# Feed-forward nets in three passes of 256 columns, and x-side tiles at another start address

## The chip, the cores and the metric

The kernel runs on one core of one Trainium2 chip. The metric is the device time of one execution in microseconds (us); 1 us is 1000 ns. The core has a matmul engine (TensorE, PE in the profile; its weight loads stand under PEld), VectorE (DVE), ScalarE (ACT), GpSimd (POOL) and SyncE (SP, which here issues the transfers of the weights). Matmul operands are read from the on-chip memory SBUF, which has 128 partitions, and sums are gathered in PSUM banks of 512 float32 columns.

## The reference

A sequence of 256 positions of width 1024 runs through two blocks of two layers each. In the first block a layer is a mixer (pooling with attention, then a gated recurrence) and a feed-forward net; in the second block it is three attentions with gates, a feed-forward net and a gated side input. Everything is float32. The two nets, cut to what matters:

```
def conv_ffn(h, w_in, conv_w, conv_b, w_out):            # first block, 2 layers
    z = causal_dwconv(h @ w_in, conv_w, conv_b)          # h: 256 x 1024, w_in: 1024 x 5632
    u, g = jnp.split(z, 2, axis=-1)
    return (jax.nn.gelu(g) * u) @ w_out                  # w_out: 2816 x 1024

# second block, 2 layers
h = rms_norm_2(x, g_ffn)
a = depthwise_conv(h @ w_ffn_gate, conv_w, conv_b)       # 1024 x 2816
x = x + (jax.nn.gelu(a) * (h @ w_ffn_up)) @ w_ffn_down
```

## The kernel before

Every float32 product is made of three passes with operands in a rounded format (float32r): each operand is split into a high and a low part, and the sum is high*high + high*low + low*high. `mm3` (L277 to L281) issues the three, one line each: L279, L280, L281. One matmul has a stationary operand of 128x128, which a weight load brings into the array ahead of it, and a moving operand of up to 512 columns that streams past it.

The weights come as one stream of chunks of up to 128x2048, in the order of use. `_push` (L245 to L267) takes one chunk: SP issues the transfer into a tile `st`, ACT rounds it to `hi` (L262), DVE writes the rest to `lo` (L263), each in two halves. There are three buffers of each kind, and up to three chunks are prepared ahead of use (`AHEAD`).

On the other side of a product stands a tile with the normed activations. Before the change it is called `xx`: for each of 8 groups of 128 channels it holds 256 columns of high parts and, right behind them, 256 columns of low parts. `norm` and `first_norm` fill it and return its two halves `xh` and `xl`. The gated attention output (`o`, later again `xx`) and the hidden values of the nets (`hg`) are split in the same way. The text calls all of these the x-side tiles.

Two kinds of product occur. In a feature-major one (`fm_pair`, `fm_first`, `gate`, `branch`) the weights are stationary and the x-side tile moves, 256 columns a pass. In a token-major one (`tm_wide`, `tm_block`) the x-side tile is stationary and the weights move, mostly 512 columns a pass.

A net (`ffn`) has 22 blocks of 128 u and 128 g columns. A block is one chunk, 2 x 8 products of 128x128 by 256 columns, so 48 matmuls of 256 columns into one bank, T and S in turn. Then follow the norm's factor (`times_r`, DVE), the convolution, the gelu, the product with u and a split into `hg`. After every second block a token-major run `tm_wide` of 24 matmuls of 512 columns adds two blocks' share of the output to four banks A, A, A, O. The first two blocks of a net come together in `fm_first`, before the norm's factor is known.

In the two nets of the second block (`ffn_b`) blocks 3 to 17 take another form, `fm_wide` (L602 to L612): the high part of a weight moves past once with 512 columns, xh and xl together (L610), and the low part with the 256 columns of xh (L611). The 32 matmuls of such a block go into two banks, one of T and one of S, and `join` (L614 to L622) adds the two halves of each bank: two copies by ACT (L619), two adds by DVE (L620) and one multiply by DVE (L621).

Each tile tag has a fixed place in SBUF, given in the order in which tags are first used. `start` uses all large tags once, in a written order, so that order sets their addresses. Modulo 512 bytes per partition `st`, `hi` and `lo` start at 448. Behind them the small tags `ssx`, `ess` and `trcos` push the next ones on: `xx`, `w4`, `o`, `hg`, `w6`, `s`, `pT`, `qk`, `w2` and `bias` start at 128. A weight slice of 128 columns is 512 bytes and 256 columns are 1024, so slices of most chunks and all slices of x-side tiles keep these remainders. The exception is the chunk of 416 columns in `mla_prep`, whose rows are 1664 bytes, that is 3 x 512 + 128: its four groups of channels start at 448, 64, 192 and 320.

The order of the work on an engine is set by a scheduler from the program's order and its dependencies; in the attention part PE keeps the written order.

Of the kernel before, what the change touches and what calls it, by code (L numbers as in the profile page):

```python
# [12 lines left out]
F32R = mybir.dt.float32r  # L13
I32 = mybir.dt.int32
AF = mybir.ActivationFunctionType
ALU = mybir.AluOpType
# [3 lines left out]
P = 128  # L20
S = 256
D = 1024
KD = D // P
DFF = 2816
NF = DFF // P
# [4 lines left out]
CHUNK = 2048  # L30
# [179 lines left out]
class Net:  # L210
# [127 lines left out]
    def update(self, t, n, banks):  # L338
        xs = self.x[:, t, n * 512:n * 512 + 512]
        if banks is not None:  # L340
            self.nc.vector.tensor_tensor(out=xs, in0=banks[t][n][:, :], in1=xs, op=ALU.add)

    def first_norm(self):

        nc = self.nc
        self.xx = self.t([P, KD, 2 * S], "xx", F32R)
        xh, xl = self.xx[:, :, :S], self.xx[:, :, S:]
        ss = self.t([P, 2, 2], "ssx")
        copies = []
        for n in range(2):  # L350
            for t in range(2):
                pt = self.bank("ST"[t])
                for e in range(4):
                    k = 4 * n + e
                    self.pe.transpose(pt[:, e * P:e * P + P], self.x[:, t, k * P:k * P + P], self.ident)
                for e in range(4):
                    k = 4 * n + e
                    g = self.vec("gain0", k)
                    z, c = pt[:, e * P:e * P + P], slice(t * P, t * P + P)
                    copies.append(nc.scalar.activation(xh[:, k, c], z, AF.Copy, scale=g))  # L360
                    nc.vector.scalar_tensor_tensor(xl[:, k, c], z, g, xh[:, k, c].bitcast(F32), op0=ALU.mult, op1=ALU.subtract)
        for n in range(2):
            for t in range(2):
                sq = self.t([P, 512], "w2")
                self.after(nc.scalar.activation(sq, self.x[:, t, n * 512:n * 512 + 512], AF.Square, scale=1.0 / 32,
                                                accum_out=ss[:, n, t:t + 1]), copies)
        self.norm_r(ss)
        return xh, xl

    def norm(self, gi, banks=None, update=None):  # L370


        nc = self.nc
        update = update or self.update
        self.xx = self.t([P, KD, 2 * S], "xx", F32R)
        xh, xl = self.xx[:, :, :S], self.xx[:, :, S:]
        ss = self.t([P, 2, 2], "ssx")
        for n in range(2):
            for t in range(2):
                update(t, n, banks)  # L380
            for kp in range(2):
                pt = self.bank("ST"[kp])
                for e in range(2):
                    k = 4 * n + 2 * kp + e
                    for t in range(2):
                        self.pe.transpose(pt[:, e * S + t * P:e * S + t * P + P], self.x[:, t, k * P:k * P + P], self.ident)
                for e in range(2):
                    k = 4 * n + 2 * kp + e
                    g = self.vec(f"gain{gi}", k)
                    z = pt[:, e * S:e * S + S]  # L390
                    nc.scalar.activation(xh[:, k, :], z, AF.Copy, scale=g)  # L391
                    nc.vector.scalar_tensor_tensor(xl[:, k, :], z, g, xh[:, k, :].bitcast(F32), op0=ALU.mult, op1=ALU.subtract)
        for n in range(2):
            for t in range(2):
                sq = self.t([P, 512], "w2")
                nc.scalar.activation(sq, self.x[:, t, n * 512:n * 512 + 512], AF.Square, scale=1.0 / 32, accum_out=ss[:, n, t:t + 1])
        self.norm_r(ss)
        return xh, xl
# [48 lines left out]
    def start(self):  # L447
        nc, ap = self.nc, self.ap
        self.vecs = self.t(list(ap["vec"].shape), "vec")
        self.ident = self.t([P, P], "ident")  # L450
        g0 = self.vat["gain0"]
        self.act_o.dma_start(self.ident, ap["ident"])
        self.act_o.dma_start(self.vecs[:, g0:g0 + KD], ap["vec"][:, g0:g0 + KD])
        self.x = self.t([P, 2, D], "x")
        for tag, n in (("st", CHUNK), ("hi", CHUNK), ("lo", CHUNK), ("ssx", 4), ("ess", 4), ("trcos", 32)) + (("xx", 4 * D), ("w4", D), ("o", D), ("hg", 512), ("w6", 1536), ("s", 512), ("pT", 512), ("qk", 512), ("w2", 512), ("bias", 512)):
            self.t([P, n], tag)
        self.sync_o.dma_start(self.x[:, 0, :], ap["x"][:P, :])
        for _ in range(3):
            self._push()
        self.rows = self.t(list(ap["row"].shape), "row")  # L460
        self.ones = self.t([P, P], "ones")
        self.sync_o.dma_start(self.vecs[:, g0 + KD:], ap["vec"][:, g0 + KD:])
        self.sync_o.dma_start(self.ones, ap["ones"])
        self.sync_o.dma_start(self.rows, ap["row"])
        self.acc = None
# [133 lines left out]
        self.fm_pair(b, xh, xl, wh, wl, KD)  # L599
        return b  # L600

    def fm_wide(self):  # L602

        banks = [self.bank(tag) for tag in "TS"]
        wh, wl = self.chunk(KD, 256)
        mm = self.pe.matmul
        for e in range(2):
            for k in range(KD):
                c = slice(e * P, e * P + P)
                mm(banks[e], wh[:, k, c], self.xx[:, k, :], start=k == 0, stop=False)  # L610
                mm(banks[e][:, :S], wl[:, k, c], self.xx[:, k, :S], start=False, stop=k == KD - 1)  # L611
        return banks  # L612

    def join(self, z, banks):  # L614

        nc = self.nc
        y = self.t([P, 2, S], "w2")
        for e, b in enumerate(banks):
            nc.scalar.activation(y[:, e, :], b[:, S:], AF.Copy)  # L619
            nc.vector.tensor_tensor(out=z[:, e, :], in0=b[:, :S], in1=y[:, e, :], op=ALU.add)  # L620
        nc.vector.tensor_tensor(out=z, in0=z, in1=self.rb[:, None, :].to_broadcast([P, 2, S]), op=ALU.mult)  # L621
        return z  # L622

    def times_r(self, z, src):

        nc = self.nc
# [5 lines left out]
                                    in1=self.rb[:, None, :].to_broadcast([P, 2, S]), op=ALU.mult)  # L632
        return z

    def ffn(self, gi, body, aside=None, wide=False):
        xh, xl = self.norm(gi, self.acc)
        first = self.fm_first(xh, xl)
        self.norm_rows()
        acc = None
        done = []  # L640
        for j in range(NF):
            if aside is not None and 2 <= j < NF - 2:
                next(aside, None)
            if j % 2 == 0:
                hh, hl = self.t([P, 2, S], "hg", F32R), self.t([P, 2, S], "hg", F32R)
                done.append((hh, hl))
            z = self.t([P, 2, S], "s")
            if wide and 3 <= j < NF - 4:
                self.join(z, self.fm_wide())
            else:  # L650
                self.times_r(z, first[j] if j < 2 else self.fm(xh, xl, "TS"[j % 2]))
            m = body(j, z[:, 0, :], z[:, 1, :])
            self.split(hh[:, j % 2, :], hl[:, j % 2, :], m)
            if j % 2 and j > 2 * LAG:
                if acc is None:
                    acc = self.wide_banks()
                kk = j - 1 - 2 * LAG
                self.tm_wide(acc, *done[kk // 2], kk, False)
        for kk in range(NF - 2 * LAG, NF, 2):
            self.tm_wide(acc, *done[kk // 2], kk, kk == NF - 2)  # L660
        self.acc = acc
# [13 lines left out]
    def ffn_b(self, i, gi, aside):  # L675
        nc = self.nc

        def body(j, u, g):
            g = self.conv(g, f"cw{i}", f"cb{i}", j, 3, (1, 0, -1))
            nc.scalar.activation(g, g, AF.Gelu_apprx_tanh)  # L680
            nc.vector.tensor_tensor(out=g, in0=g, in1=u, op=ALU.mult)
            return g

        self.ffn(gi, body, aside, True)


    def softplus(self):
# [559 lines left out]
    def hybrid(self, i, g0):  # L1247
        nc = self.nc
        xh, xl = self.norm(g0, self.acc, self.pending)
        c, kr, skr = self.mla_prep(i, xh, xl)  # L1250
# [40 lines left out]

        def branch(b):
            if b == 2:
                mm = self.t([P, KD, 2 * S], "xx", F32R)
                mh, ml = self.halves = mm[:, :, :S], mm[:, :, S:]
            for jp in range(4):
                if jp % 2 == 0:
                    wh, wl = self.chunk(4, 512)
# [31 lines left out]
        for _ in branch(2):  # L1330
            pass
        mh, ml = self.halves
# [22 lines left out]
        xh, xl = self.norm(g0 + 2, self.acc)  # L1355
# [4 lines left out]
        e = [self.t([P, D], "w4") for _ in range(2)]  # L1360
# [10 lines left out]
        for t in range(2):  # L1371
            for n in range(2):
                c = slice(n * 512, n * 512 + 512)
# [49 lines left out]
```

## Time and profile before

| what | value |
|---|---|
| device time, median of 3 runs | 1484.84 us (1483.95 to 1485.08) |
| the profiled execution's own time | 1484.23 us |
| its span, first to last instruction | 1482.3 us |
| PE, PEld, DVE, ACT, POOL busy | 99%, 89%, 78%, 63%, 7% |
| matmuls | 9540 |
| mean DMA rate | 174 GB/s |
| granted TensorE clock | full (2.4 GHz) in every slice |

A matmul's duration in the profile includes a fixed latency; matmuls overlap. What a matmul costs the engine is the distance from its start to the next one's start, here called its pitch. A view of one matmul per row gives it, as the distance of two rows divided by the matmuls between them. The chain of waits is the list of steps, each released by the one before, that ends with the last instruction.

### The profile page before, as it was taken

What the parts mean: (1) busy time and instruction counts of PE and PEld (TensorE: products, weight loads), DVE (VectorE), ACT (ScalarE), POOL (GpSimd) and SP (SyncE); (2) the same over time, 40 slices, a digit from 0 to 9 for tenths busy, and PEclk for the clock granted to TensorE, in tenths of its full rate; (3) what the DMA queues carried; (4) which work ended last, traced back from release to release, by engine and by line L of the source; (5) the groups of instructions that cost most, each with busy time, mean ns of one, the idle gap of its engine ahead of it and who ended that gap; (6) DMA issues with size and microseconds to landing.
All of it is one profiled execution on the core that took longest, in us unless ns stands there. A gap on an engine that the chain in (4) does not pass through costs nothing.

```text
span 1482.3 us, 24541 instructions
## 1 busy us (share of the span) xinstructions
PE 1469.4 (99%) x9540; PEld 1312.3 (89%) x9540; DVE 1160.1 (78%) x2257; ACT 934.1 (63%) x1684; POOL 106.9 (7%) x101
## 2 busy tenths in 40 slices
PE   8999999999999999999999999999999999999998
PEld 6689999999999998899998988888899998988896
DVE  6669777789897877886877877778886877877766
ACT  7757555586666556765765755656766664765554
POOL 0200000000000000012530000000003250000000
PEclk9999999999999999999999999999999999999999
DMA  8455455444455554543335555544443435555551
GB/s 296 159 187 200 174 197 198 166 149 171 161 209 174 196 182 157 199 170 116 142 116 192 180 206 183 199 171 171 168 179 133 136 121 172 192 197 178 191 199 57
DMA packets 37877, 257.29 MB, mean 174 GB/s; under 512 B 4385, under 2 KB 4769, under 8 KB 8321
## 3 DMA queue, kind: packets, MB, share of 16 engines
q1 hardware_dynamic: 36576, 252.38, 47.9%
q0 software_dynamic: 896, 3.28, 0.6%
q8 instruction: 75, 1.23, 0.3%
q14 instruction: 42, 0.34, 0.1%
q10 hardware_dynamic: 288, 0.07, 0.0%
HBM read 254.66 MB, written 1.05 MB: 173 GB/s over the span
## 4 chain that ended last, share of the span: by engine, by line
PE 87%; DVE 8%; ACT 3%; issue 2%; DMA 0%; ACTq 0%
PE A L207 11%; PE A L280 9%; PE A L279 9%; PE A L281 9%; PE S L279 4%; PE S L281 4%; PE S L280 4%; PE T L279 4%; PE T L281 4%; PE T L280 4%; PE S L610 4%; PE T L610 4%; DVE lo L263 3%; PE T L611 2%; PE S L611 2%
## 5 line engine op out<-in xcount | busy, mean ns | idle before, releaser
L263 DVE TENSOR_TENSOR lo<-st,hi 128x1024 fp32r<-128x1024 f32 (+3 forms) x480 | 574.7, 1211 | 136.4 <-ACT hi L262 135.6
L262 ACT ACTIVATE hi<-st 128x1024 fp32r<-128x1024 f32 (+3 forms) x480 | 489.8, 1042 | 228.2 <-PE A L207 60.3
L281 PE MATMUL S<-xx,lo 128*128 128x256 f32 x496 | 139.4, 281 | 0.0
L279 PE MATMUL S<-xx,hi 128*128 128x256 f32 x496 | 139.2, 281 | 0.0
L280 PE MATMUL S<-xx,hi 128*128 128x256 f32 x496 | 139.1, 281 | 0.0
L207 PE MATMUL A<-xx,hi 128*128 128x256 f32 x768 | 138.8, 284 | 0.0
L279 PE MATMUL T<-xx,hi 128*128 128x256 f32 x480 | 135.6, 283 | 0.0
L280 PE MATMUL T<-xx,hi 128*128 128x256 f32 x480 | 135.0, 281 | 0.0
L281 PE MATMUL T<-xx,lo 128*128 128x256 f32 x480 | 134.8, 281 | 0.0
L207 PEld LDWEIGHTS A<-xx,hi 128*128 128x128 f32 x768 | 117.0, 188 | 8.2 <-issue 7.9
L281 PE MATMUL A<-hi,hg 128*128 128x512 f32 x294 | 115.6, 393 | 0.6 <-DVE hg L314 0.6
L279 PE MATMUL A<-hi,xx 128*128 128x512 f32 (+2 forms) x304 | 115.8, 383 | 0.2 <-ACT xx L391 0.2
L280 PE MATMUL A<-lo,hg 128*128 128x512 f32 x294 | 115.6, 393 | 0.0
L280 PE MATMUL A<-lo,xx 128*128 128x512 f32 (+2 forms) x304 | 115.3, 379 | 0.1
L279 PE MATMUL A<-hi,hg 128*128 128x512 f32 x294 | 115.1, 391 | 0.0
L281 PE MATMUL A<-hi,xx 128*128 128x512 f32 (+2 forms) x304 | 114.5, 379 | 0.0
L207 PE MATMUL A<-xx,lo 128*128 128x256 f32 x384 | 107.1, 279 | 0.0
L1115 POOL TENSOR_SCALAR s<-s,at 128x256 f32<-128x256 f32 x56 | 55.2, 1003 | 571.4 <-DVE at L960 570.8
L281 PEld LDWEIGHTS S<-xx,lo 128*128 128x128 f32 x496 | 94.6, 191 | 0.1
L279 PEld LDWEIGHTS S<-xx,hi 128*128 128x128 f32 x496 | 93.2, 188 | 0.1
L280 PEld LDWEIGHTS S<-xx,hi 128*128 128x128 f32 x496 | 93.2, 188 | 0.1
L281 PEld LDWEIGHTS T<-xx,lo 128*128 128x128 f32 x480 | 91.8, 191 | 0.0
(377 smaller groups left out, 3458.0 us busy)
## 6 DMA issues: line engine op xcount, KB each, us to landing
st<-in_w_dram SPq DMA_DIRECT2D x230, 1024.0 KB, 4.8
st<-in_w_dram SPq DMA_DIRECT2D x4, 832.0 KB, 4.9
st<-in_w_dram SPq DMA_DIRECT2D x2, 768.0 KB, 4.2
x<-in_x_dram SPq DMA_DIRECT2D x2, 512.0 KB, 5.1
st<-in_w_dram SPq DMA_DIRECT2D x4, 256.0 KB, 6.7
st<-in_w_dram SPq DMA_DIRECT2D x2, 512.0 KB, 3.5
w<-in_gain_dram POOLq DMA_DIRECT2D x2, 512.0 KB, 4.4
out_dram<-x SPq DMA_DIRECT2D x4, 256.0 KB, 2.0
```

The costliest lines, as they stand in the source:

```text
L207: return lambda *a, **k: self.tc.keep_in_program_order(f(*a, **k))
L262: nc.scalar.activation(hi[:, c0:c1], st[:, c0:c1], AF.Copy)
L263: nc.vector.tensor_tensor(out=lo[:, c0:c1], in0=st[:, c0:c1], in1=hi[:, c0:c1].bitcast(F32), op=ALU.subtract)
L279: mm(out, ah, bh, start=start, stop=False)
L280: mm(out, ah, bl, start=False, stop=False)
L281: mm(out, al, bh, start=False, stop=stop)
L610: mm(banks[e], wh[:, k, c], self.xx[:, k, :], start=k == 0, stop=False)
L611: mm(banks[e][:, :S], wl[:, k, c], self.xx[:, k, :S], start=False, stop=k == KD - 1)
L1115: nc.gpsimd.tensor_scalar(s[:, c], s[:, c], r[:, t:t + 1], None, op0=ALU.mult)
```

## The change

It has two parts. `fm_wide` and `join` are gone, and all blocks of all nets use three passes of 256 columns (`fm`, `times_r`). And the tile `xx` is replaced by two tiles, `xh` and `xl`, of 256 columns by 8 groups each; the small tags ahead of them are now `trcos` and `trsin`, so all x-side tiles start at 192 modulo 512 in place of 128. `st`, `hi` and `lo` stay at 448.

```diff
@@ first_norm, and the same in norm
-        self.xx = self.t([P, KD, 2 * S], "xx", F32R)
-        xh, xl = self.xx[:, :, :S], self.xx[:, :, S:]
+        xh = self.t([P, KD, S], "xh", F32R)
+        xl = self.t([P, KD, S], "xl", F32R)
@@ start
-        for tag, n in (("st", CHUNK), ("hi", CHUNK), ("lo", CHUNK), ("ssx", 4), ("ess", 4), ("trcos", 32)) + (("xx", 4 * D), ("w4", D), ...
+        for tag, n in (("st", CHUNK), ("hi", CHUNK), ("lo", CHUNK), ("trcos", 32), ("trsin", 32)) + (("xh", 2 * D), ("xl", 2 * D), ("w4", D), ...
@@
-    def fm_wide(self):
-        banks = [self.bank(tag) for tag in "TS"]
-        wh, wl = self.chunk(KD, 256)
-        mm = self.pe.matmul
-        for e in range(2):
-            for k in range(KD):
-                c = slice(e * P, e * P + P)
-                mm(banks[e], wh[:, k, c], self.xx[:, k, :], start=k == 0, stop=False)
-                mm(banks[e][:, :S], wl[:, k, c], self.xx[:, k, :S], start=False, stop=k == KD - 1)
-        return banks
-    def join(self, z, banks):
...
@@ ffn
-            z = self.t([P, 2, S], "s")
-            if wide and 3 <= j < NF - 4:
-                self.join(z, self.fm_wide())
-            else:
-                self.times_r(z, first[j] if j < 2 else self.fm(xh, xl, "TS"[j % 2]))
+            z = self.times_r(self.t([P, 2, S], "s"), first[j] if j < 2 else self.fm(xh, xl, "TS"[j % 2]))
@@ hybrid, branch
-                mm = self.t([P, KD, 2 * S], "xx", F32R)
-                mh, ml = self.halves = mm[:, :, :S], mm[:, :, S:]
+                mh, ml = self.halves = self.t([P, KD, S], "xh", F32R), self.t([P, KD, S], "xl", F32R)
```

On PE, where block 2 of the first `ffn_b` ends and block 3 begins, there stands before (T is a bank, `hi` and `lo` are weights):

```order
L279 MATMUL T_1355_9073<-xx_1316_8853,hi_1333_8922 128x256
L280 MATMUL T_1355_9073<-xx_1316_8853,hi_1333_8922 128x256
L281 MATMUL T_1355_9073<-xx_1316_8853,lo_1334_8923 128x256
L610 MATMUL T_1365_9150<-xx_1316_8853,hi_1336_8930 128x512
L611 MATMUL T_1365_9150<-xx_1316_8853,lo_1337_8931 128x256
L610 MATMUL T_1365_9150<-xx_1316_8853,hi_1336_8930 128x512
L611 MATMUL T_1365_9150<-xx_1316_8853,lo_1337_8931 128x256
```

At the same place there stands now:

```order
L279 MATMUL T_1362_9080<-xh_1322_8859,hi_1340_8929 128x256
L280 MATMUL T_1362_9080<-xl_1323_8860,hi_1340_8929 128x256
L281 MATMUL T_1362_9080<-xh_1322_8859,lo_1341_8930 128x256
L279 MATMUL S_1372_9157<-xh_1322_8859,hi_1343_8937 128x256
L280 MATMUL S_1372_9157<-xl_1323_8860,hi_1343_8937 128x256
L281 MATMUL S_1372_9157<-xh_1322_8859,lo_1344_8938 128x256
```

Each pair of a 512 and a 256 column matmul has become three of 256 columns, and block 3 fills one bank S in place of a T and an S. The places of the token-major runs between the blocks, and PE's order outside these blocks, are the same.

On DVE, at the same block 3, there stands before (`s` is the block's result, `w` the copy by ACT, `rb` the norm's factor):

```order
L681 TENSOR_TENSOR pT_1359_9131<-pT_1359_9131,s_1354_9072 128x256
L620 TENSOR_TENSOR s_1364_9149<-T_1365_9150,w_5_1370_9192 128x256
L263 TENSOR_TENSOR lo_1384_9224<-st_1382_9221,hi_1383_9223 128x1024
L314 TENSOR_TENSOR hg_1353_9071<-pT_1359_9131,hg_1352_9070 128x256
L207 TENSOR_TENSOR lampr_1360_9139<-row_29_115 128x64
L620 TENSOR_TENSOR s_1364_9149<-S_1366_9151,w_5_1370_9192 128x256
L207 TENSOR_REDUCE sm_5_1361_9140<-lampr_1360_9139 128x1
L621 TENSOR_TENSOR s_1364_9149<-s_1364_9149,rb_1344_9042 128x512
```

And now:

```order
L655 TENSOR_TENSOR pT_1366_9138<-pT_1366_9138,s_1361_9079 128x256
L609 TENSOR_TENSOR s_1371_9156<-S_1372_9157,rb_1351_9049 128x512
L263 TENSOR_TENSOR lo_1388_9240<-st_1386_9237,hi_1387_9239 128x1024
L314 TENSOR_TENSOR hg_1360_9078<-pT_1366_9138,hg_1359_9077 128x256
L207 TENSOR_TENSOR lampr_1367_9146<-row_29_115 128x64
```

The two adds L620 are gone, and the multiply by `rb` reads the bank itself (L609, which was L631).

## Rows read from the trace of the kernel before

**Rows 1.** The page: span, then busy us, share and instructions by engine.

```profile
span 1482.3 us, 24541 instructions
PE 1469.4 (99%) x9540; PEld 1312.3 (89%) x9540; DVE 1160.1 (78%) x2257; ACT 934.1 (63%) x1684; POOL 106.9 (7%) x101
...
PEclk9999999999999999999999999999999999999999
```

**Rows 2.** The page: chain that ended last, share of the span by engine.

```profile
PE 87%; DVE 8%; ACT 3%; issue 2%; DMA 0%; ACTq 0%
```

**Rows 3.** Busy time of each engine in a stretch of a first-block net.

```profile
core 0: us, PE busy (x) PEld busy (x) DVE busy (x) ACT busy (x) POOL busy (x), PEclk, DMA share, GB/s
402.00:570.00 168.00, 168.00 (x1178) 156.99 (x1177) 139.25 (x253) 103.39 (x158) 3.69 (x2) 1.00 0.54 188
```

**Rows 4.** Timeline, PE, first-block net: 48 matmuls of one T block (start, duration).

```profile
206.65 0.28 PE L279 MATMUL T<-xx,hi 128*128 128x256 f32 x1
...
212.31 0.28 PE L279 MATMUL S<-xx,hi 128*128 128x256 f32 x1
```

**Rows 5.** Timeline, PE, end of a second-block net: blocks 18 (T) and 19 (S).

```profile
949.86 0.28 PE L279 MATMUL T<-xx,hi 128*128 128x256 f32 x1
...
955.33 0.28 PE L279 MATMUL S<-xx,hi 128*128 128x256 f32 x1
...
960.77 0.39 PE L279 MATMUL A<-hi,hg 128*128 128x512 f32 x1
```

**Rows 6.** Timeline, PE, second-block net: one wide block, 16 pairs.

```profile
832.26 0.40 PE L610 MATMUL T<-xx,hi 128*128 128x512 f32 x1
...
837.91 0.40 PE L610 MATMUL T<-xx,hi 128*128 128x512 f32 x1
```

**Rows 7.** Timeline, PE: first of the 24 matmuls of 512 before Rows 4.

```profile
201.14 0.40 PE L279 MATMUL A<-hi,hg 128*128 128x512 f32 x1
```

**Rows 8.** Groups by line and form in 290:297.5 and in 206.8:212 (busy us, mean ns).

```profile
L281 PE MATMUL S<-xx,lo 128*128 128x256 f32 x14 | 3.9, 276 | 0.0
...
L281 PE MATMUL T<-xx,lo 128*128 128x256 f32 x15 | 4.2, 281 | 0.0
```

**Rows 9.** Groups by line and form, whole span: third passes of 256 columns.

```profile
L281 PE MATMUL S<-xx,lo 128*128 128x256 f32 x496 | 139.4, 281 | 0.0
...
L281 PE MATMUL T<-xx,lo 128*128 128x256 f32 x480 | 134.8, 281 | 0.0
...
L207 PE MATMUL A<-xx,lo 128*128 128x256 f32 x384 | 107.1, 279 | 0.0
...
L207 PE MATMUL A<-o,lo 128*128 128x256 f32 x128 | 35.7, 279 | 0.0
...
L281 PE MATMUL A<-xx,lo 128*128 128x256 f32 x112 | 31.0, 279 | 0.0
...
L281 PE MATMUL A<-o,lo 128*128 128x256 f32 x64 | 17.7, 277 | 0.0
```

**Rows 10.** Groups by line: chunk of 416 columns, its four channel groups, 577.68 on.

```profile
L280 PE MATMUL A<-lo,xx 128*128 128x416 f32 x1 | 0.4, 353 | 0.0
...
L280 PE MATMUL A<-lo,xx 128*128 128x416 f32 x1 | 0.3, 350 | 0.0
...
L280 PE MATMUL A<-lo,xx 128*128 128x416 f32 x1 | 0.4, 354 | 0.0
...
L279 PE MATMUL A<-hi,xx 128*128 128x416 f32 x1 | 0.3, 350 | 0.0
```

**Rows 11.** Groups by line and form, whole span: what joins a wide block's halves.

```profile
L621 DVE TENSOR_TENSOR s<-s,rb 128x512 f32<-128x512 f32 x30 | 20.6, 685 | 0.0
...
L620 DVE TENSOR_TENSOR s<-T,w 128x256 f32<-128x256 f32 x30 | 12.5, 418 | 0.0
...
L619 ACT ACTIVATE w<-T 128x256 f32<-128x256 f32 x30 | 11.4, 381 | 14.7 <-PE T L611 14.7
```

**Rows 12.** Groups by line and form, whole span: 512-column matmuls, two of the groups.

```profile
L279 PE MATMUL A<-hi,hg 128*128 128x512 f32 x294 | 115.1, 391 | 0.0
...
L610 PE MATMUL S<-xx,hi 128*128 128x512 f32 x240 | 86.1, 398 | 0.0
```

More of the change, by code (lines that the diff above doesn't have):

```diff
@@ L374, in norm @@
         update = update or self.update
-        self.xx = self.t([P, KD, 2 * S], "xx", F32R)
-        xh, xl = self.xx[:, :, :S], self.xx[:, :, S:]
+        xh = self.t([P, KD, S], "xh", F32R)
+        xl = self.t([P, KD, S], "xl", F32R)
         ss = self.t([P, 2, 2], "ssx")
@@ L454, in start @@
         self.x = self.t([P, 2, D], "x")
-        for tag, n in (("st", CHUNK), ("hi", CHUNK), ("lo", CHUNK), ("ssx", 4), ("ess", 4), ("trcos", 32)) + (("xx", 4 * D), ("w4", D), ("o", D), ("hg", 512), ("w6", 1536), ("s", 512), ("pT", 512), ("qk", 512), ("w2", 512), ("bias", 512)):
+        for tag, n in (("st", CHUNK), ("hi", CHUNK), ("lo", CHUNK), ("trcos", 32), ("trsin", 32)) + (("xh", 2 * D), ("xl", 2 * D), ("w4", D), ("o", D), ("hg", 512), ("w6", 1536), ("s", 512), ("pT", 512), ("qk", 512), ("w2", 512), ("bias", 512)):
             self.t([P, n], tag)
@@ L600, in fm @@
         return b
-    def fm_wide(self):
-        banks = [self.bank(tag) for tag in "TS"]
-        wh, wl = self.chunk(KD, 256)
-        mm = self.pe.matmul
-        for e in range(2):
-            for k in range(KD):
-                c = slice(e * P, e * P + P)
-                mm(banks[e], wh[:, k, c], self.xx[:, k, :], start=k == 0, stop=False)
-                mm(banks[e][:, :S], wl[:, k, c], self.xx[:, k, :S], start=False, stop=k == KD - 1)
-        return banks
-    def join(self, z, banks):
[L616 to L622, printed above, removed]
     def times_r(self, z, src):
@@ L633, in times_r, with ffn @@
         return z
-    def ffn(self, gi, body, aside=None, wide=False):
+    def ffn(self, gi, body, aside=None):
         xh, xl = self.norm(gi, self.acc)
@@ L682, in body @@
             return g
-        self.ffn(gi, body, aside, True)
+        self.ffn(gi, body, aside)
     def softplus(self):
```

## The prediction

> **What bounds the kernel now.** I read the page's busy shares first: PE is busy for 99% of the span, at the full granted clock (2.4 GHz) in every slice [rows 1]. The chain that ended last agrees: 87% of it is PE [rows 2]. In a stretch of a first-block net PE is busy for all 168.00 us, while DVE has 139.25, ACT 103.39 and the transfers run at 0.54 of their engines [rows 3]. So time is saved or lost by the pitch of the matmuls, and the question is what sets that.
>
> The timeline gives the pitch. One block of 48 matmuls of 256 columns runs from 206.65 to 212.31 us, 5.66 us, or 118 ns each [rows 4]. The same form with the same tiles at the same remainders, at the end of a second-block net, runs from 955.33 to 960.77, 5.44 us, or 113.3 ns [rows 5]. The narrow form thus has two pitches, a long one (118 ns) and a short one (113.3 ns); a block keeps the one it is in. The block before that one, from 949.86, takes 5.47 us [rows 5]: a few matmuls at the long pitch behind a run of 512 columns, then the short one, 0.03 us in all. A wide block takes 5.65 us for 16 pairs [rows 6], 353 ns a pair. A narrow triple at the long pitch is 5.66/16 = 354 ns, at the short one 5.44/16 = 340 ns. The wide form is worth no more than narrow passes at the long pitch.
>
> **How much of the kernel has the long pitch.** A matmul's duration is its pitch plus a constant: a stretch at the short pitch shows 276 ns, one at the long pitch 281 [rows 8], 5 ns apart as the pitches are. So the mean duration of a group tells its mixture. I take the third pass of each triple, because it rarely has a wait in front of it [rows 9], and 276.5 as the short end, between the 276 and 277 that groups at the short pitch show. With (mean - 276.5)/5 the shares at the long pitch are 0.9 of 496, 0.9 of 480, 0.5 of 384, 0.5 of 128, 0.5 of 112 and 0.1 of 64 triples: 446 + 432 + 192 + 64 + 56 + 6 = 1196 long triples out of 1664. The means are rounded to 1 ns, which leaves this some 160 off either way.
>
> **The change part by part.** (1) The wide form goes. There are 15 blocks of 16 pairs in two nets, 480 pairs, as the groups of L610 show (240 in S [rows 12], as many in T). Each becomes a triple: at the long pitch 480 x (354 - 353) = +0.5 us, at the short one 480 x (340 - 353) = -6.2 us.
>
> (2) Two ACT copies and two DVE adds per wide block go: 60 x 0.37 = 22 us of ACT and 60 x 0.418 = 25 us of DVE [rows 11]. The multiply stays, reading a bank in place of SBUF, at the same 0.685 us or so. All of this lies beside PE, which does not wait in the nets, so I cost it at nothing; bounds are 0 and a gain of under 1 us at the ends of the two nets, where the last block's result is awaited. No wait, queue or transfer is added: SP's and POOL's orders keep their rows.
>
> (3) The addresses. The chunk of 416 columns tells that they matter. It moves past x-side tiles that start at 128; its four groups start at 448, 64, 192 and 320. Their durations are 353, 350, 354 and 350 ns [rows 10]. Moving minus stationary, modulo 256, is 64, 192, 64 and 192: a distance of 64 costs 3 to 4 ns a matmul more than 192, and a period of 256 bytes fits all four. Before the change the feature-major passes have 128 - 448 = 192 modulo 256 and the token-major ones 448 - 128 = 64. Afterwards both have 256, that is 0. No steady run of these passes has a distance of 0 before, so this is the unknown. My reading: the moving stream and the weight load next to it get in each other's way when distance plus their lag in time meets a certain value. At 256 and 512 columns, whole multiples of 256 bytes, the lag repeats from matmul to matmul, hence the two lasting pitches. At 192 one value of the lag is clean and the other is not; at 64 the 416 chunk is hit. The distance 0 is 64 bytes from both places where trouble is seen. I therefore expect the narrow form at its short pitch nearly everywhere.
>
> The Trainium skill has a rule against this: SBUF — State Buffer, section on the two separate sides, holds that only the port pair which VectorE and GpSimd share causes contention on the engine side, and that PE never waits on anyone. By it alone the remainder could not matter; the four durations of the 416 chunk [rows 10] disagree.
>
> In numbers: 1196 long triples become short, 1196 x 13.5 = -16.1 us (the 13.5 lies between 354 - 340 = 14 and 3 x (281 - 276.5) = 13.5, on the lower side). With the -6.2 us of the wide form that is -22.3. What stays long are the entries: 0.03 us for each run of 256 columns that follows 512 columns or a wait. I count about 90 of them (9 in each of four nets, the rest gates and branches of the second block), +2.7 us. The token-major matmuls of 512 columns take 212.31 - 5.66 = 206.65 to 201.14 [rows 4, 7], 5.51 us for 24, 229.6 ns. I leave them as they are. Bounds: twice the short 256-column pitch, 226.7 ns, or the wide form's 353 - 118 = 235 ns. The trace has 2303 of them (294 in the largest group [rows 12]), so -6.7 to +12.4 us. The sum is -22.3 + 2.7 = -19.6 us on the profiled execution's 1484.2, so 1464.6; the median of the runs is 0.6 above that execution: 1465.2, which I round to 1466 because some of the gain in the attention part will meet other waits.
>
> The model in one line: there are 1664 + 480 = 2144 triples after; a wide pair counts as long, so before has (1196 + 480)/2144 = 0.78 of them long, and the change is worth 2144 x 13.5 ns = 28.9 us times (long share after - 0.78).
>
> **Rivals.** First, the addresses do nothing and the pitch is set by what comes before a block. Then the second-block nets behave like the first-block ones, at the long pitch from block 2 to the end: the wide form's +0.5 us, and the eight short-pitch blocks at the ends of the two nets (8 x 0.21 = +1.7 us) are lost. 1484.8 + 2.2 = 1487, within the bound of no change. For it: 0.9 of the narrow triples in T and S are long, although nothing but their neighbours differs from the short ones. Against: rows 10. The isolated gap in TensorE: Matmul & The Clock Gate, section on the back-to-back issue gap, of the same Trainium skill (columns divided by 2.4, plus 2.5 ns) would make three passes of 256 columns 327.5 ns and the pair 325.0, an estimate of +1.2 us for the 480; the measured pitches are 3 to 9% over it.
>
> Second, the pitches stay mixed, at about 0.4 long: -0.38 x 28.9 = -11, 1474. For it: the gates and branches are a half-and-half mixture now, by what precedes them.
>
> Third, slower: 0 modulo 256 is a place of conflict for both kinds of pass, at every lag. Then all 2144 triples are long, +0.22 x 28.9 = +6.4 us, and the 512-column passes go to 235 ns, up to +12.4: 1491 to 1504. It decides from a long share above 0.78. For it: no row excludes it, and the token-major side's remainder moves as well. Against: equal remainders modulo 256 would have to be bad at once for two kinds of pass whose distances 64 and 192 behave differently now.
>
> **How the numbers follow.** I give the short pitch nearly everywhere 0.5 (1459 to 1473), the mixture 0.15 (around 1474), no effect 0.18 (around 1487), slower 0.17 (1491 to 1504). What a measurement can tell from no change is 0.2%, 3 us. So faster is 0.5 + 0.15 less a little, 0.64; same takes most of the no-effect case and a sliver of the mixture, 0.18; slower 0.18. The range 1458 to 1491 leaves out 0.05 below and about 0.15 above.
>
> **What would show it.** Right: mean durations of 276 to 277 ns in the groups of rows 9; a narrow block of 5.44 us in a first-block net, where rows 4 have 5.66; the second-block nets' blocks 3 to 17 likewise; the 416 chunk, whose groups then stand at distances of 0 and 128, with all four near 350. Wrong: means of 281 in S and T (no effect, or a longer time), or a 512-column group at 398 in place of 391. If the means are right and the time is not, a wait on DVE or the weight stream has taken PE's place, and PE's busy share would fall below 99%.

## The result: 1.2% slower

The changed kernel takes 1501.67 us, the median of 4 runs (1501.45 to 1501.85), against 1484.39 us before (4 runs, 1476.78 to 1485.08): a ratio of 1.0119, with a 95% interval of 1.0105 to 1.0132. Forecast were 1466 us, in a range of 1458 to 1491, and a gain. The rival that ends slower gave 1491 to 1504.

The page of the kernel after, its span and its busy times, stands against [rows 1]:

```profile
span 1500.1 us, 25361 instructions
PE 1486.8 (99%) x10020; PEld 1355.5 (90%) x10020; DVE 1141.0 (76%) x2197; ACT 918.5 (61%) x1626; POOL 108.1 (7%) x101
...
PEclk9999999999999999999999999999999999999999
```

PE is still busy for 99%, at the full granted clock, so nothing has taken its place: its own matmuls have become longer. Without the join DVE and ACT are busy for 19 and 16 us less, and it bought nothing.

The timeline of PE in a first-block net of the kernel after (start, duration; a run of 24 matmuls of 512 columns, a T block, an S block, the next run) answers to [rows 4, 7]:

```profile
202.90 0.40 PE L279 MATMUL A<-hi,hg 128*128 128x512 f32 x1
...
208.37 0.28 PE L279 MATMUL T<-xh,hi 128*128 128x256 f32 x1
...
214.12 0.28 PE L279 MATMUL S<-xh,hi 128*128 128x256 f32 x1
...
219.88 0.40 PE L279 MATMUL A<-hi,hg 128*128 128x512 f32 x1
...
875.36 0.28 PE L279 MATMUL T<-xh,hi 128*128 128x256 f32 x1
...
881.12 0.28 PE L279 MATMUL S<-xh,hi 128*128 128x256 f32 x1
```

The S block is 219.88 - 214.12 = 5.76 us for 48 matmuls: 120.0 ns. This is a third pitch. Before there were 118 and 113.3 ns [rows 4, 5]. The last two rows are a second-block net, in a place where a wide block stood: 5.76 us again, for 5.65 [rows 6]. The run of 512 columns ahead takes 208.37 - 202.90 = 5.47 us, 228 ns each, for 229.6 [rows 4, 7]: shorter.

The groups of third passes of the kernel after, one of 512 columns, and one of weight loads:

```profile
L281 PE MATMUL S<-xh,lo 128*128 128x256 f32 x752 | 213.2, 283 | 0.0
L281 PE MATMUL T<-xh,lo 128*128 128x256 f32 x704 | 199.2, 283 | 0.0
L280 PE MATMUL A<-lo,hg 128*128 128x512 f32 x294 | 114.8, 391 | 0.0
L207 PE MATMUL A<-xh,lo 128*128 128x256 f32 x384 | 108.5, 283 | 0.0
L207 PE MATMUL A<-o,lo 128*128 128x256 f32 x128 | 36.1, 282 | 0.0
...
L281 PEld LDWEIGHTS S<-xh,lo 128*128 128x128 f32 x752 | 144.4, 192 | 0.1
```

Every group of 256 columns that showed 277 to 281 ns [rows 9], a mixture of the two pitches, is at 282 or 283, the gates and branches of the attention part (A) included. There is no mixture left. By their starts, all 80 blocks of the four nets behind the first two of each settle at 120.0 ns (mean over the second half of a block); before the change 42 of the 50 narrow ones settled at 117.8 and the 8 at the ends of the second-block nets at 113.3.

Summing the distances from one start to the next in the two traces (those with a stop in them set apart) accounts for the whole difference of the spans, 1500.1 - 1482.3 = 17.8 us:

| matmuls | before | after | difference |
|---|---|---|---|
| 256 columns, x-side halves, narrow already | 4333 at 116.46 ns | 119.89 ns | +14.9 us |
| 256 columns, o tiles | 556 at 114.66 | 119.70 | +2.8 |
| 480 wide pairs, now triples | 353.2 | 359.8 | +3.2 |
| 512 columns but those of the wide form, with their stops | 535.0 us | 531.7 us | -3.3 |
| all else | | | +0.2 |

### The profile page after: what moved, and what is told of

It reads as the page before. It is cut to its first block, busy times and chain, and to the rows that moved or that the text cites. A ratio compares the mean times of both kernels' runs of the same rounds, so it can differ in the third digit from the quotient of the medians.

```text
span 1500.1 us, 25361 instructions
## 1 busy us (share of the span) xinstructions
PE 1486.8 (99%) x10020; PEld 1355.5 (90%) x10020; DVE 1141.0 (76%) x2197; ACT 918.5 (61%) x1626; POOL 108.1 (7%) x101
## 4 chain that ended last, share of the span: by engine, by line
PE 85%; DVE 9%; ACT 3%; issue 2%; DMA 0%; SPq 0%; ACTq 0%
PE A L207 11%; PE A L279 8%; PE A L280 8%; PE A L281 8%; PE S L279 6%; PE S L281 6%; PE S L280 6%; PE T L281 6%; PE T L280 6%; PE T L279 6%; DVE lo L263 4%; PE T L207 2%; PE S L207 2%; PE O L281 2%; PE O L280 2%
## 5 line engine op out<-in xcount | busy, mean ns | idle before, releaser
L263 DVE TENSOR_TENSOR lo<-st,hi 128x1024 fp32r<-128x1024 f32 (+3 forms) x480 | 573.7, 1209 | 122.1 <-ACT hi L262 119.2
L281 PE MATMUL S<-xh,lo 128*128 128x256 f32 x752 | 213.2, 283 | 0.0
L280 PE MATMUL S<-xl,hi 128*128 128x256 f32 x752 | 213.0, 283 | 0.0
L279 PE MATMUL S<-xh,hi 128*128 128x256 f32 x752 | 213.0, 283 | 0.0
L279 PE MATMUL T<-xh,hi 128*128 128x256 f32 x704 | 199.8, 284 | 0.0
L280 PE MATMUL T<-xl,hi 128*128 128x256 f32 x704 | 199.4, 283 | 0.0
L281 PE MATMUL T<-xh,lo 128*128 128x256 f32 x704 | 199.2, 283 | 0.0
L281 PEld LDWEIGHTS S<-xh,lo 128*128 128x128 f32 x752 | 144.4, 192 | 0.1
L279 PEld LDWEIGHTS S<-xh,hi 128*128 128x128 f32 x752 | 144.4, 192 | 0.1
L280 PEld LDWEIGHTS S<-xl,hi 128*128 128x128 f32 x752 | 144.4, 192 | 0.1
L279 PEld LDWEIGHTS T<-xh,hi 128*128 128x128 f32 x704 | 135.0, 192 | 1.3
```

What stands on the lines that cost most here:

```text
L263: nc.vector.tensor_tensor(out=lo[:, c0:c1], in0=st[:, c0:c1], in1=hi[:, c0:c1].bitcast(F32), op=ALU.subtract)
L279: mm(out, ah, bh, start=start, stop=False)
L280: mm(out, ah, bl, start=False, stop=False)
L281: mm(out, al, bh, start=False, stop=stop)
```

## The experiments

The theories were: A, the remainder of the distance (moving minus stationary start, modulo 256 bytes) sets the pitch; B, the form of the blocks or the other engines do; C, the period is 512 bytes. P (several stable pitches at one distance) came up with the second sweep.

**A sweep of distances, TensorE alone (sweep).** 

> Computes nothing of the reference: x goes out as it came. PE alone, in long blocks: for each distance d (start of the moving operand minus start of the stationary one, 0 to 496 bytes in steps of 16) first 24 matmuls of 512 columns at the distance -d, then 48 of 256 columns at d, from otherwise idle engines. Theory A (the remainder of that distance modulo 256 sets the pitch): 120 ns at 0 and 256, 113 or 118 at 192 and 448, the same pattern in both halves; 512 columns 227 ns at 0, about 229 at a distance of 64. Theory B (the three-pass form or what other engines do sets it, not the address): one pitch, 113 or 118, at all distances. Theory C (the period is 512): 0 and 256 differ. Four more blocks at the end alternate 0 and 128 bytes: moving and stationary together, against each other, the stationary alone, the moving alone; if a matmul's own two operands count, together is as d = 0 and against as d = 128; if the moving operand and the next weight load count, the other way round.

```
for d in range(0, 128, 4):          # 16 bytes a step, 512 bytes in all
    run(d)                          # 24 x 512 columns: weights move, x stands
    narrow(d)                       # 48 x 256 columns: x moves, weights stand
```

The timeline of the sweep, one row for each group; the distance from one group's start to the next is what the group took. The three groups of 48 are at distances 112, 192 and 256, which is 0 again:

```profile
96.92 5.68 PE L45 MATMUL N<-xt,w 128*128 128x256 f32 x48
102.43 5.74 PE L45 MATMUL R<-w,xt 128*128 128x512 f32 x24
...
153.04 5.62 PE L45 MATMUL N<-xt,w 128*128 128x256 f32 x48
158.50 5.72 PE L45 MATMUL R<-w,xt 128*128 128x512 f32 x24
...
197.48 5.91 PE L45 MATMUL N<-xt,w 128*128 128x256 f32 x48
203.23 2.03 PE L45 MATMUL R<-w,xt 128*128 128x512 f32 x8
```

5.75 us at distance 0, 5.46 at 192, 5.51 at 112: with nothing but TensorE and an eviction per bank at work, the address alone makes 120.0 or 113.3 ns (means over the second half of a group). The second 256 bytes of the sweep repeat the first within 0.1 ns, and its weights start at 128 modulo 256, where the kernel's start at 192: it is the distance that counts, with a period of 256. A holds; B and C do not. The whole table, in ns; the three columns for 256 are from the second sweep (below), and the 512-column pass of a row stands at minus the row's distance, so its own 64 is in row 192:

```
distance of the    256 columns, behind            512 columns, the same
256-column pass    512 at 0   512 at 64   a stop  tiles with roles swapped
   0                120.0      120.0      120.0      226.7
  16                118.7      118.7      118.7      233.3
  32                116.7      116.7      116.7      233.2
  48                118.3      118.3      118.3      233.3
  64                117.8      117.8      117.8      233.4
  80                120.0      118.3      118.3      232.0
  96                120.0      120.0      120.0      234.3
 112                113.3      113.3      113.3      233.3
 128                120.0      120.0      118.6      232.4
 144                116.7      116.7      118.8      233.4
 160                118.5      118.8      117.4      233.4
 176                119.4      119.2      119.4      230.0
 192                117.8      113.3      117.8      228.9
 208                119.2      119.2      119.2      232.0
 224                118.3      118.3      118.3      233.5
 240                117.0      117.3      117.1      228.4
```

Distance 0 is the best place of all for 512 columns and one of the worst for 256. The sweep's last four groups, which shift every other operand by 128 bytes, were to tell whether a matmul's moving reads meet its own load or the next one: moving and stationary together gave 116.7, against each other 116.7, stationary alone 118.3, moving alone 116.7. Each of the two pairings asked for 120.0 in one of the first two groups, so neither fits as it stands.

**The form alone (narrow128).** 

> The changed kernel with its x-side tiles back at 128: the form of the change without its addresses. Theory A: the two pitches of before return (118 and 113.3 ns, in 512 columns 229), time 1478 to 1487. Theory B: all stays at 120 ns, 1501.

```diff
-("lo", CHUNK), ("trcos", 32), ("trsin", 32)) + (("xh", 2 * D), ...
+("lo", CHUNK), ("ssx", 4), ("ess", 4), ("trcos", 32)) + (("xh", 2 * D), ...
```

1486.73 us (10 runs), ratio to before 1.0015 (1.0002 to 1.0027): +2.2 us. The timeline of a first-block net in this kernel:

```profile
206.81 0.28 PE L279 MATMUL T<-xh,hi 128*128 128x256 f32 x1
...
212.46 0.28 PE L279 MATMUL S<-xh,hi 128*128 128x256 f32 x1
```

5.65 us a block, as in [rows 4]. So the form is close to nothing, and the rest of the loss is the address's. Every block behind the first two of a net is now at 117.8 ns, 80 of 80, in all four nets, the ones at the end, short before [rows 5], included: this is what the first rival said of the form by itself, 1487.

**The address alone (wide192).** 

> The kernel before with its x-side tiles at 192: the addresses of the change without its form. Theory A: narrow blocks at 120 ns as after, 512 columns at 227; if that also holds for the 512 columns of the wide form, its pair takes 347 ns in place of three passes of 360, so 480 x 13 = 6 us less than the changed kernel, about 1495. Theory B: 1484 as before.

```diff
 # the kernel before, wide blocks kept
-("lo", CHUNK), ("ssx", 4), ("ess", 4), ("trcos", 32)) + (("xx", 4 * D), ...
+("lo", CHUNK), ("trcos", 32), ("trsin", 32)) + (("xx", 4 * D), ...
```

1498.95 us, ratio 1.0095 (1.008 to 1.011): +14.1 us, without touching an instruction. The first-block net of this kernel:

```profile
208.57 0.28 PE L279 MATMUL T<-xx,hi 128*128 128x256 f32 x1
...
214.32 0.28 PE L279 MATMUL S<-xx,hi 128*128 128x256 f32 x1
```

5.75 us a block: the new pitch comes with the address. The 2.7 us left to the changed kernel go with its 480 triples at 359.8 ns, where the pairs have 352.9 here (480 x 6.9 = 3.3 us). Theory A's 347 for the pair, and with it its 1495, did not come.

**Another distance (narrow64).** 

> The changed kernel with its x-side tiles at 64, a distance of 128 modulo 256 for both kinds of pass. Theory A has no number for it: as 0 if only equal distances of both kinds count (1501), below 1484 if 128 is the point farthest from the conflict at 0. Theory B: 1501.

```diff
-("lo", CHUNK), ("trcos", 32), ("trsin", 32)) + (("xh", 2 * D), ...
+("lo", CHUNK), ("trcos", 32)) + (("xh", 2 * D), ...
```

With the halves at 64 both kinds of pass are at distance 128: 1506.16 us, ratio 1.0144 (1.0129 to 1.0159). The trace's mean pitches are 118.9 ns for 256 columns and 232.5 to 232.8 for 512; the sweep has 118.6 to 120.0 and 232.4. The blocks of the four nets settle at 118.5 to 118.8 ns (60 of 80) or at 120.0 (20). None of the expected times came: the 256 columns are a little shorter than at 0, and the 512 columns some 5 ns longer. This is the third rival's picture, both kinds hurt at once, but at another address than the change's.

**What stands before a block (sweep2).** 

> A kernel of matrix products alone (its output is not the reference's, all its products are thrown away): runs of 24 512-column matmuls and groups of 48 256-column matmuls in triples, as in the nets. First part: each of 16 distances (moving minus stationary start, modulo 256 bytes, steps of 16) behind a 512-column run at distance 0, behind one at distance 64, and behind a stop of the engine. Theory P (at a given distance there are several stable pitches, and what stood before chooses): at 192 at least one of the three entries gives 117.8 ns, another 113.3; at 0 all three give 120. Theory Q (the distance alone sets the pitch): the three entries agree within 0.3 ns at every distance, 192 at 113.3. Second part: the low halves are moved by 0, 64, 128, 192 bytes against the high ones on both sides, at base distances 192, 112 and 0. Theory R (each load is paired with the moving operand that runs beside it, so the mean over three pairs counts): mixtures lie between 113.3 and 120; a pitch below 113 would speak for a better arrangement than any single distance.

```
for e in (0, 48):                   # distance of the run ahead: 0, then 64 modulo 256
    for d in range(0, 64, 4):
        run(e); narrow(d)
for d in range(0, 64, 4):
    narrow(d, tag="G", bufs=1)      # one bank: the engine stops ahead of each group
```

The timeline of this sweep, distance 192: behind a run at 0, behind a run at 64, behind another run at 64 (second part, low halves not shifted), behind a stop; and distance 112 behind a stop. N groups are followed by the start of the next group:

```profile
152.42 5.82 PE L43 MATMUL N<-xt,w 128*128 128x256 f32 x48
158.07 2.20 PE L43 MATMUL R<-w,xt 128*128 128x512 f32 x9
...
331.12 5.62 PE L43 MATMUL N<-xt,w 128*128 128x256 f32 x48
336.58 1.76 PE L43 MATMUL R<-w,xt 128*128 128x512 f32 x7
...
476.68 5.82 PE L43 MATMUL N<-xt,w 128*128 128x256 f32 x48
482.34 5.72 PE L43 MATMUL R<-w,xt 128*128 128x512 f32 x24
...
446.34 5.92 PE L43 MATMUL G<-xt,w 128*128 128x256 f32 x48 [0.43 <-ACT junk L46]
...
414.64 5.77 PE L43 MATMUL G<-xt,w 128*128 128x256 f32 x48 [0.43 <-ACT junk L46]
```

At distance 192 the same 48 matmuls take 5.65 us or 5.46, by what stood before: two lasting pitches at one address, theory P. Q falls. The run just ahead does not settle which: behind a run at 64 the same block took 5.46 us in the first part and 5.66 in the second (482.34 - 476.68), and in narrow128, behind runs at 64, all 80 blocks are at 117.8. What in the work before decides is not shown. Distance 208 has two pitches as well: 119.2 in the table, 116.7 in the first sweep. Distance 112 has one only: behind each of the three entries, and in the first sweep, it settles at 113.3 ns within 9 to 15 matmuls. Distance 0 has one too, 120.0. The part with the low halves shifted against the high ones gave 113.3 to 121.1 ns, nothing below 113.3, and no rule of means is seen: from the bases 0, 192 and 112, shifting both low halves by 128 bytes gave 117.8, 120.4 and 116.7. Theory R is not borne out.

**One kind of tile moved (narrow_hg192).** 

> The changed kernel with its x-side tiles back at 128 modulo 512 (256-column distance 192, as before) and only the hg tiles, which are nothing but stationary operands of the 512-column products of the nets, at 192 (512-column distance 0). Against the same kernel with hg at 128 too (1486.7 us): theory A (the remainder of the distance sets the pitch, per kind of pass) expects the 1176 matmuls with hg at 226.7 to 227.5 in place of 229.2, which is -2.0 to -2.9 us: 1484 us if the 256-column blocks behind them stay at 117.8 ns; and if the new entry turns them to 113.3 ns, up to 24 blocks x 96 x 4.5 ns more per pair of nets, 10 us less in all: 1474. A theory by which the whole layout or the other engines' tiles matter, and not this distance, expects no change: 1486.7.

```diff
 # on top of narrow128
-("o", D), ("hg", 512), ("w6", 1536), ...
+("o", D), ("sm1", 1), ("sm2", 1), ("hg", 512), ("posq", 2), ("posqf", 2), ("trsin", 32), ("w6", 1536), ...
```

1484.21 us (10 runs), ratio 0.9997 (0.9987 to 1.0007), which is 2.5 us below narrow128: theory A's 1484. A run of 24 matmuls with hg, and the block behind it:

```profile
201.97 0.39 PE L279 MATMUL A<-hi,hg 128*128 128x512 f32 x1
...
207.41 0.28 PE L279 MATMUL T<-xh,hi 128*128 128x256 f32 x1
...
213.07 0.28 PE L279 MATMUL S<-xh,hi 128*128 128x256 f32 x1
```

The run takes 5.44 us, 226.7 ns each, and the block 5.66: distance 0 helps the one, and the entry behind it still leads to 117.8 ns, in all 80 blocks.

**A start for each use (split112).** 

> The changed kernel (1501.7 us) with the start of each pair of x-side halves chosen by its use: halves that are moving operands of 256-column passes are taken 112 bytes further on (distance 112 from the weights), halves that are only stationary operands of 512-column products stay at distance 0, hg at distance 0, the o tiles at 128 modulo 256 as before. Theory P (remainder of the distance, with several stable pitches at some distances and one alone, 113.3 ns, at 112): the 5856 passes that read xh or xl go from 120.0 to 113.3 ns, -39 us, of which some 50 entries with eleven passes near 118.5 ns each give back 3; the 576 passes on o tiles -3; the 384 512-column and 96 416-column matmuls of the two attention stages whose halves serve both uses +3. In all -36: 1466 us, clearly below the kernel before (1484.8). Theory E (what stands before a block decides in the kernel, as it did at distance 192): part of the blocks lock at 117.8 or longer, 1480 to 1490. Theory O (another engine is next: VectorE at 76% of the span with waits for evictions): the matmul pitch falls to 113.3 but the gaps between blocks grow, 1475 to 1485.

```diff
 # the changed kernel; a tile is 256 (xh) or 192 bytes (xl) larger than its half; the small tags
 # between the large ones, which set the starts of hg and o, are left out here
+    def half(self, tag, shift):
+        b = self.t([P, 2 * D + self.PAD[tag]], tag, F32R)
+        return b[:, shift:shift + 2 * D].rearrange("p (k s) -> p k s", k=KD)
-        xh = self.t([P, KD, S], "xh", F32R)
-        xl = self.t([P, KD, S], "xl", F32R)
+        xh, xl = self.half("xh", shift), self.half("xl", shift)   # 28 words, or 0 where only stationary
```

1468.84 us (5 runs, 1468.13 to 1469.31), ratio 0.9902 (0.9884 to 0.9919): faster than both kernels, 15.5 us below before. The hg tiles are at 192, as in the changed kernel, and the o tiles at 128, as before it. Lines of its page, then the timeline of a first-block net:

```profile
span 1467.5 us, 25361 instructions
PE 1452.3 (99%) x10020; PEld 1318.3 (90%) x10020; DVE 1139.1 (78%) x2197; ACT 918.5 (63%) x1626; POOL 107.2 (7%) x101
...
L287 PE MATMUL S<-xh,lo 128*128 128x256 f32 x752 | 207.3, 276 | 0.0
...
L287 PEld LDWEIGHTS S<-xh,lo 128*128 128x128 f32 x752 | 141.2, 188 | 0.1
```

```profile
198.80 0.39 PE L285 MATMUL A<-hi,hg 128*128 128x512 f32 x1
...
204.27 0.28 PE L285 MATMUL T<-xh,hi 128*128 128x256 f32 x1
...
209.75 0.28 PE L285 MATMUL S<-xh,hi 128*128 128x256 f32 x1
...
215.19 0.39 PE L285 MATMUL A<-hi,hg 128*128 128x512 f32 x1
```

The S block takes 5.44 us, the short pitch, and the T block in front of it 5.48, its entry. The mean duration is 276 ns. All 80 blocks settle at 113.3 ns. Theory P holds, E and O fall: PE's share stays at 99%. It is 3 us over the expected 1466: the mean pitch of the passes on x halves is 114.0 ns, 0.7 over the short one, where the entries had been put at 0.5, and the runs with hg are at 227.7, as in the changed kernel, and not at 226.7. These two make some 2 of the 3 us.

**The form at the short pitch (wide112).** 

> The kernel before, wide blocks and all, with the starts chosen by use as in split112: feature-major halves 112 bytes beyond the weights' remainder, halves that are only stationary at 0, hg at 0, o as before. It asks what the form of a block is worth where the 256-column pitch is short. Theory F (step 1 of the prediction: a wide pair keeps its 353 ns, a triple is 3 x 113.3 = 340): 480 pairs x 13 ns = 6 us more than split112, 1475 us. Theory G (a wide pair too goes by the distance of its own operands, and its 512-column half moves what a triple's first two passes move): a pair at 340 to 347 ns, 0 to 3 us more than split112, 1469 to 1472. Theory H (distance 112 is bad for the 512-column half, as it was at 233.3 ns where weights moved and x stood): a pair at 347 to 353, 1472 to 1475. The mean pitch of the wide blocks in the trace tells G from H and F.

```diff
 # the kernel before, wide blocks kept; starts as in split112
-        self.xx = self.t([P, KD, 2 * S], "xx", F32R)
+        self.xx = self.both(shift)          # [P, 4 * D + 48], 28 words on or 0
```

1474.34 us (6 runs), ratio 0.9937 (0.9925 to 0.995), 5.5 us over split112. A wide block of its second-block net:

```profile
829.55 0.40 PE L614 MATMUL T<-xx,hi 128*128 128x512 f32 x1
...
832.37 0.40 PE L614 MATMUL S<-xx,hi 128*128 128x512 f32 x1
```

Eight pairs in 2.82 us, 353 ns a pair as before. Theory G falls. F and H both allow for this pair and this time, and this run does not part them; but a wide pair has nearly the same mean at three distances, 353.2 ns at 192, 352.9 at 0 (wide192) and 353.1 at 112, which is F's picture.

## Why the prediction was wrong

**What bounds the kernel** was right: PE is at 99% in every kernel with the nets, and the sums of the pitches give the change's whole difference of time.

**Two pitches and their shares** were right: the starts give a mean of 116.46 ns over the passes that were narrow already, which is 0.70 of them long; read from mean durations it was 1196/1664 = 0.72.

**Step 1, the form,** was right in its prices and wrong in which one applied. At the short pitch the triples are worth 5.5 us (wide112 against split112), forecast 6.2; at the long one nothing, +2.2 us with the ends of the nets (narrow128), where the first rival had +0.5 and +1.7. The change ran at neither, and paid 3.2 us.

**Step 2, the join,** was right where it counts: PE gained nothing. The busy times of ACT and DVE fell by 16 and 19 us, where the sums of the rows' durations had given 22 and 25.

**Step 3, the addresses, is the step that failed,** in the sentence "The distance 0 is 64 bytes from both places where trouble is seen. I therefore expect the narrow form at its short pitch nearly everywhere." Of the two places, 192 was known from the blocks of 256 columns and 64 from the chunk of 416 [rows 10], and 0, which no row had, was read as clean because it lies between. In the changed kernel that chunk does as foretold: its durations are some 350 ns at distance 0 and 351 at 128, no worse than before. But what a distance costs a pass of one width need not hold for another: the sweep has 226.7 ns for 512 columns at 0, its best, and 120.0 for 256 columns, as long as at any distance of the table. Even 416 and 512 columns differ: 64 is dearer than 192 for the one [rows 10], and for the other it has 228.9 ns against 233.4. And a distance between two known ones cannot be interpolated: 16 bytes to either side of 112 (113.3 ns) lie 120.0 at 96 and 118.6 to 120.0 at 128. The two pitches that the step chose between were those of 192; 0 has one of its own, a longer one, and no entry changes it. So the term that stood as -16.1 us, with +2.7 for entries, was +17.7 (14.9 and 2.8 of the ledger), and the wide form's -6.2 was +3.2.

**The 512-column passes,** left as they were with bounds of -6.7 to +12.4, gained 3.3 us. The third rival was right that all triples become long, and its 1491 to 1504 holds the time; but its mechanism, one conflict for both kinds of pass, is not what happened, so that its range holds the time is in part luck. It had the triples at 354 ns and the loss in the 512 columns; in fact the triples went to 360 and the 512 columns went the other way.

**The first rival,** that addresses do nothing, is excluded: sweep and wide192 change nothing else. In the sweep no other engine is at work beyond an eviction, and by where the moving columns and the weights start against each other the pitch of 256 columns still differs by 6% (113.3 to 120.0 ns). The Trainium skill, SBUF — State Buffer, section on the two separate sides, holds that PE never waits on anyone; read as in the prediction, so that the start addresses could not matter, this rule does not hold for these passes. The rival's half of truth is that what comes before a block chooses among the pitches, which sweep2 shows at 192 and a few other distances.

What stays open is why. That the pitch goes by the distance, with a period of 256 bytes, and is the same for weights at 128 and at 192 modulo 256, is shown. Which read meets which load is not: the alternating groups and the shifted low halves fit neither simple pairing.

## What to carry to other kernels

Where one engine sits at 99%, read its pitch from start to start before anything else, and treat the start addresses of its operands as a parameter to be measured: a sweep of one run gave the table that two rows of the old trace could not. Measure each width of pass by itself, since the best distance for one can be the worst for another, and choose a tile's start by its use; a view some words into a slightly larger tile is enough. Prefer a distance at which every entry settles at the same pitch over one that is good only behind some neighbours.

## What the runs showed that was not expected

A distance can have more than one lasting pitch, chosen by what stood before, and such kernels scatter more: nine runs of the kernel before lay between 1479.93 and 1485.97 us and ten of narrow128 between 1481.88 and 1488.86, but four of the changed kernel between 1501.45 and 1501.85, and five of split112, whose halves all stand at distance 112 or 0, between 1468.13 and 1469.31. That blocks change their pitch from run to run is the likely reason, but it is not shown: there is one trace of each kernel.

The weight loads differ too, but they do not give the pitch away: their mean is 192 ns in the groups that stand at 120.0 ns and 188 in the same groups of split112, at 113.3; in narrow128, where every block is at 117.8, it is 188 for the first two passes of a triple in S and 191 for the third.
